# Stacked F32R attention scores with a reordered first mixer, and a second feed-forward that applies the norm's root after its projection

## The chip, the cores and the metric

The kernel runs on one core of one Trainium2 chip. The metric is the device time of one execution in microseconds; less is better. TensorE is called PE here, VectorE DVE, ScalarE ACT, as the profile names them.

## What is computed

Two layers of a hybrid backbone work on 256 latent tokens and 256 context tokens of width 1024. Layer 0 mixes with differential attention (4 heads) and a bidirectional gated linear attention (4 heads), layer 1 with a bidirectional HGRN2 (8 heads). Each layer has a SwiGLU feed-forward of width 2816, and each sub-layer an RMS norm with a scale and a shift from the conditioning vector. Only the latent rows leave layer 1. Cut to what the change touches:

```python
def diff_attend(q, k, v, lam):
    s = jnp.einsum('bqhcd,bkhcd->bhcqk', q, k).astype(F32) * (A_DQK ** -0.5)   # A_DQK = 64, c = 2 channels
    p = jax.nn.softmax(s, axis=-1)
    a = (p[:, :, 0] - lam * p[:, :, 1]).astype(v.dtype)
    return jnp.einsum('bhqk,bkhe->bqhe', a, v)
...
ol = jnp.concatenate([post_a(oa_l), post_b(ob_l, bgl)], axis=-1)     # post_b: rms_norm(o) * silu(g)
x = x + mod_l[2] * (ol @ w_out)
hl = rms_norm(x, norm2_gain[l]) * (1.0 + mod_l[4]) + mod_l[3]
x = x + mod_l[5] * swiglu(hl, w_ffn_in[l], w_ffn_out[l])             # (silu(hl @ Wg) * (hl @ Wu)) @ Wo
```

## The kernel before

Features lie on the 128 partitions (8 tiles `k` of 1024 features), tokens along the free dimension: columns 0 to 255 are context, 256 to 511 latents. Large matrices are multiplied at F32 quality from two F32R parts: a weight piece of 128 x 1024 (8 blocks) comes in as `w`, ACT rounds it to `wH`, DVE makes the rest `wL = w - wH` (`wpiece`, L270 and L271). The activations are split in the same way (`hH`, `hL`). `mm3` then issues three products for a block: `wH` by the high part, `wH` by the low part, `wL` by the high part. `dense_group` loops over `k`, and for each `k` over the output tiles; `dense_wide`, used by layer 1's feed-forward alone, puts a row's high and low part side by side in one 512-column operand, so that a block takes a pair of products, of 512 and of 256 columns, and the two halves of the 512-column result are added later.

A Tile scheduler sets the order on every engine from the program's order, priorities and its own estimate of times; each engine then runs its own list strictly in order. So a product that waits holds back all that stands behind it on PE. Buffers come from pools; those of a tag with one buffer are reused only when the last reader is done. The PSUM pools hold three banks of tag `d` (`dtile`), and two each of tags `a` and `s` and one of `t` (`mtile`).

The first mixer: `qk_tile(which, hd)` projects one head's queries or keys (24 products of 512 columns, except for head 0), takes their mean squares with a product by `c_blk64` (L744), the root by Ln and Exp on ACT, and rotates the latent half. It leaves one F32 tile with channel 0 on rows 0 to 63 and channel 1 on rows 64 to 127; each head has a tile of its own (`x0` to `x7`, the buffers of the residual stream, which is read again from memory afterwards). `attn_head(hd)` makes the scores `s_ps` (L774): context queries against 256 keys, latent queries against 512, in blocks of 128 queries, and for each block and channel one F32 product of 64 rows. DVE takes the maximum, ACT the exponential, DVE combines the channels, PE transposes (`t_ps`) and multiplies by the values (`oa_ps`). `gla_pair(p)` is the linear attention of two heads; its many tiny products (32 and 64 wide) write the tile `a`. `ada(n)` computes adaLN vectors by 32-row products of `ada_w` on PE. The output gate `gs` of the linear attention is 4 dense groups of 24 products, then copied and passed through Silu. `split` makes the high and low part of the mixer's output tiles, `oH` and `oL`; `ov[0..3]` are attention, `ov[4..7]` linear attention. The scheduler interleaves all of these.

Layer 1's end: the HGRN2 heads end with `o_ps`, a normalization on ACT (`hos`), a transposition `ot_ps`, a gate product on DVE (L1142) and the split into `ov` (L1145, L1146). The out projection takes output tiles 0 to 5 in one group and then 6 and 7 in groups of their own. `residual` (L844) adds each result to the residual stream. `token_rstd` sums squares by products with ones (`nms`) and takes the root, `norm_part` multiplies, shifts and splits into `hw`, and `ffn_narrow` starts its first group of four output tiles with `dense_wide`.

Of the kernel before, what the change touches and what calls it, by code (L numbers as in the profile page):

```python
# [51 lines left out]
def hybrid_kernel(ctx: ExitStack, tc: tile.TileContext, A, out, dbg=None):  # L52
# [752 lines left out]
    for hd in range(1, 4):  # L805
        ada(1, "d")
        qT[hd] = qk_tile(0, hd)
        kT[hd] = qk_tile(1, hd)
        ada(1, "d")
        oa[hd] = attn_head(hd)  # L810
    dump("q1", qT[1])
    dump("oa1", oa[1])
# [1 line left out]
    dump("ob1", ob[1])
    dump("ob2", ob[2])
    gs = {}
    for j in range(4):
        gs[j] = bigp.tile([P, T], F32, name=f"gs{j}", tag=f"vB{j}")
        ps = dtile()
        dense_group(fl, [ps], h, range(KT), extra=1, tag="d")  # L820
        V.tensor_copy(out=gs[j], in_=ps)
    for j in range(4):
        S.activation(out=gs[j], in_=gs[j], func=AF.Silu)
# [4 lines left out]
    for hd in range(4):
        V.tensor_tensor(out=ob[hd], in0=ob[hd], in1=gs[hd], op=ALU.mult)
        ov[4 + hd] = split(ob[hd], T, 4 + hd)  # L830
    dump("ob1p", ob[1])
# [360 lines left out]
    for j in range(6):  # L1192
        residual(o6[j], 1, 2, j, xl[j], ssq, halves(256))
# [169 lines left out]
```

## Time and profile before

| | |
|---|---|
| median of 3 runs | 1160.94 us (1158.55 to 1163.29) |
| profiled execution | 1166.56 us, its span 1164.8 us |
| mean granted PE clock | 0.988 |
| busy share PE, DVE, ACT | 98%, 70%, 48% |
| first mixer | about 93 to 303 us of the span |
| layer 0's out projection and feed-forward | about 303 to 700 us |
| layer 1's mixer | about 700 to 958 us |
| layer 1's feed-forward | 973 to 1161 us |

The profile is of one execution of the kernel. Matmuls are pipelined, so the length of one record is more than what it takes in a stream; what a product costs in a stream is the distance from its start to the next start. An F32 product leaves two records, an F32R product one.

### The profile page before, as it was taken

To read this page: it belongs to the slowest core of one execution; us is meant where nothing else is said; L and a number is where in the kernel's file an instruction comes from. 1 tells how busy PE (TensorE), PEld (TensorE's weight loads), DVE (VectorE), ACT (ScalarE), POOL (GpSimd) and SP (SyncE) were. 2 spreads that over 40 slices of the span, in tenths; PEclk is the share of its full clock that TensorE was granted. 3 is DMA by queue.
4 is the path that set the end of the run, shared out by engine and by line. 5 is a ranking of instruction groups with operands and counts; after the bars stand their busy time and mean duration, and the time that the engine had idled before them with its cause. 6 is when DMAs were issued, how large, how long until landed. Compare 5 with 4: busy or idle time off the path is not lost. (4 is left out here: it accounts for less than half of the span.)

```text
span 1164.8 us, 20915 instructions
## 1 busy us (share of the span) xinstructions
PE 1143.3 (98%) x8426; PEld 955.3 (82%) x8426; DVE 816.5 (70%) x1731; ACT 560.2 (48%) x996; POOL 0.2 (0%) x4
## 2 busy tenths in 40 slices
PE   8999989999999999999999999999999998999998
PEld 6777656666799888888888889999898987888887
DVE  3437855995668767666776647869898977776774
ACT  5435535764445222122222225858868865543552
POOL 0000000000000000000000000000000000000000
PEclk9999989999999999999999999999999998999999
DMA  9531431343433555455777521442221233556552
GB/s 359 211 116 36 147 110 37 127 145 124 146 130 109 167 192 160 153 178 181 240 238 245 177 95 55 145 145 92 73 78 69 93 128 109 184 179 199 188 193 91
DMA packets 50017, 170.13 MB, mean 146 GB/s; under 512 B 6528, under 2 KB 8064, under 8 KB 49792
## 3 DMA queue, kind: packets, MB, share of 16 engines
q1 hardware_dynamic: 49920, 168.79, 43.0%
q8 instruction: 66, 1.08, 0.4%
q14 instruction: 31, 0.25, 0.1%
HBM read 167.72 MB, written 1.05 MB: 145 GB/s over the span
## 5 line engine op out<-in xcount | busy, mean ns | idle before, releaser
L270 ACT CAST wH<-w 128x1024 fp32r<-128x1024 f32 x212 | 222.2, 1050 | 387.9 <-PE d L118 272.3
L271 DVE TENSOR_TENSOR wL<-w,wH 128x1024 fp32r<-128x1024 f32 x212 | 258.7, 1222 | 107.0 <-ACT wH L270 104.5
L118 PE MATMUL d<-hH,wH 128*128 128x512 f32 (+1 forms) x800 | 286.4, 365 | 1.6 <-DVE modt L163 1.2
L118 PE MATMUL d<-hL,wH 128*128 128x512 f32 (+1 forms) x800 | 286.2, 358 | 0.0
L118 PE MATMUL d<-hH,wL 128*128 128x512 f32 (+1 forms) x800 | 285.5, 357 | 0.0
L118 PEld LDWEIGHTS d<-hH,wH 128*128 128x128 f32 x800 | 152.1, 191 | 27.7 <-issue 2.6
L118 PEld LDWEIGHTS d<-hL,wH 128*128 128x128 f32 x800 | 151.9, 190 | 21.8 <-issue 1.2
L118 PEld LDWEIGHTS d<-hH,wL 128*128 128x128 f32 x800 | 151.5, 190 | 21.5
L118 PE MATMUL d<-hw,wH 128*128 128x512 f32 x352 | 125.9, 402 | 3.1 <-DVE hw L404 3.1
L118 PE MATMUL d<-hw,wL 128*128 128x256 f32 x352 | 99.3, 282 | 0.0
L228 DVE SCALAR_TENSOR_TENSOR jk<-ada_w,scb 128x1024 bf16<-128x1024 f32 x80 | 97.7, 1222 | 1.6 <-DMA ada_w<-in_w_ada 0.2
L118 PEld LDWEIGHTS d<-hw,wH 128*128 128x128 f32 x352 | 67.3, 191 | 19.9 <-DVE hw L404 3.5
L118 PE MATMUL d<-gH,wH 128*128 128x512 f32 (+1 forms) x198 | 72.2, 366 | 0.0
L118 PE MATMUL d<-gL,wH 128*128 128x512 f32 (+1 forms) x198 | 72.0, 365 | 0.0
L118 PE MATMUL d<-gH,wL 128*128 128x512 f32 (+1 forms) x198 | 72.0, 365 | 0.0
L118 PEld LDWEIGHTS d<-hw,wL 128*128 128x128 f32 x352 | 67.6, 192 | 0.0
L844 DVE SCALAR_TENSOR_TENSOR x<-d,modt,x 128x256 f32<-128x256 f32 x80 | 35.7, 480 | 45.2 <-PE d L118 44.9
L118 PE MATMUL d<-wH,hH 128*128 128x256 f32 (+1 forms) x192 | 61.9, 323 | 0.0
L118 PE MATMUL d<-wL,hH 128*128 128x256 f32 (+1 forms) x192 | 61.6, 322 | 0.0
L118 PE MATMUL d<-gw,wH 128*128 128x512 f32 x176 | 61.5, 396 | 0.0
L118 PE MATMUL d<-wH,hL 128*128 128x256 f32 (+1 forms) x192 | 61.5, 321 | 0.0
L947 DVE TENSOR_TENSOR fs<-fs,d 128x512 f32<-128x512 f32 (+1 forms) x24 | 15.3, 643 | 60.9 <-PE d L118 60.5
(234 smaller groups left out, 1813.7 us busy)
## 6 DMA issues: line engine op xcount, KB each, us to landing
w<-in_w_ffn_in SPq DMA_DIRECT2D x88, 512.0 KB, 3.4
ada_w<-in_w_ada SPq DMA_DIRECT2D x80, 512.0 KB, 4.3
w<-in_w_ffn_out SPq DMA_DIRECT2D x44, 512.0 KB, 3.4
ada_w<-in_w_ada SPq DMA_DIRECT2D x8, 1024.0 KB, 9.2
w<-in_w_even_a SPq DMA_DIRECT2D x16, 512.0 KB, 4.6
w<-in_w_odd_f SPq DMA_DIRECT2D x16, 512.0 KB, 3.3
x<-in_xT SPq DMA_DIRECT2D x16, 256.0 KB, 3.8
w<-in_w_out_even SPq DMA_DIRECT2D x8, 512.0 KB, 3.7
```

Of the source, the lines that this page charges most:

```text
L118: return PE.matmul(out=o, lhsT=l, rhs=r, start=start, stop=stop)
L228: ins = V.scalar_tensor_tensor(out=jk, in0=w1[0], scalar=1.0, in1=scb[:, v, :], op0=ALU.mult, op1=ALU.mult, accum_out=modt[:, l, m, dt, v: ...
L270: cast = S.copy(out=wH, in_=w)
L271: ins = V.tensor_tensor(out=wL, in0=w, in1=wH, op=ALU.subtract)
L844: tail[0] = V.scalar_tensor_tensor(out=xt[:, lo:hi], in0=ps[:, lo:hi], scalar=mods[l, m, k][:, v:v + 1], in1=xt[:, lo:hi], op0=ALU.mult, o ...
L947: V.tensor_tensor(out=s[:, lo:hi], in0=s[:, lo:hi], in1=pu, op=ALU.mult)
```

## The change

1. Scores. `qk_tile` now splits its result: for channel `c`, `qs[c]` holds the rounded queries of the channel on its own 64 rows and their remainder on the other 64 rows; `kh[c]` holds the rounded keys on both row halves, `kl[c]` the remainder on both. A score is `qs[c]` by `kh[c]` plus `qs[c]` by `kl[c]`, two F32R products over 128 rows. For the queries that is one ACT copy and one DVE subtraction of 64 rows and 512 columns per channel, for the keys two and two. These six tiles have one buffer each for all heads (tags `x0` to `x5`), and the F32 result has one per `which` (`x6`, `x7`).
2. Order of the first mixer. Attention of heads 1 and 2, then head 3's queries and keys, then `gla_pair(1)`, then all of `gs`, with attention of head 3 after that in the program but at a raised priority. `gs` is now x times Exp(-Ln(1 + Exp(-x))), without Silu. The linear attention's outputs are gated and split first, and the out projection of layer 0 takes its `k` in the order 4 to 7, 0 to 3.
3. Layer 1's out projection is one group over all eight output tiles. After each residual, ACT and DVE make `hu`: the residual stream times the norm's per-feature scale, split into a high and a low part, without the root. Two more columns of `hu`, 256 and 257, hold the shift.
4. `ffn_narrow` projects `hu` with `dense_group`: three products of 258 columns for each block. The root is computed beside the first group. `act` multiplies the 256 columns by the root on DVE and adds column 256 as the shift's projection: as the bias of Silu for the gate, as the first scalar of the product for the other half.

```diff
-        t = xp.tile([P, T], F32, name=f"qk{which}{hd}", tag=f"x{2 * hd + which}")
+        t = xp.tile([P, T], F32, name=f"qk{which}{hd}", tag=f"x{6 + which}")
...
+        for c in range(2):
+            own, far = (slice(0, 64), slice(64, 128))[::1 - 2 * c]
+            if which == 0:
+                a = xp.tile([P, T], F32R, name=f"qs{c}", tag=f"x{c}")
+                S.copy(out=a[own], in_=t[own])
+                V.tensor_tensor(out=a[far], in0=t[own], in1=a[own], op=ALU.subtract)
+                parts.append(a)
+            else:
+                a = xp.tile([P, T], F32R, name=f"kh{c}", tag=f"x{2 + 2 * c}")
+                b = xp.tile([P, T], F32R, name=f"kl{c}", tag=f"x{3 + 2 * c}")
+                for r in (own, far):
+                    S.copy(out=a[r], in_=t[own])
+                for r in (own, far):
+                    V.tensor_tensor(out=b[r], in0=t[own], in1=a[own], op=ALU.subtract)
+                parts.append((a, b))
+        return parts
...
-                    mm(sp_[:, 0:nkeys], q[r, q0:q0 + P], k[r, 0:nkeys], True, True)
+                    for i in range(2):
+                        mm(sp_[:, 0:nkeys], q[c][:, q0:q0 + P], k[c][i][:, 0:nkeys], i == 0, i == 1)
...
+            S.activation(out=e, in_=ps, func=AF.Exp, scale=-1.0)
+            V.tensor_scalar(out=e, in0=e, scalar1=2.0 ** 63, scalar2=None, op0=ALU.min)
+            S.activation(out=e, in_=e, func=AF.Ln, bias=one_t)
+            S.activation(out=e, in_=e, func=AF.Exp, scale=-1.0)
+            V.tensor_tensor(out=e, in0=ps, in1=e, op=ALU.mult)
...
     gla_pair(1)
+    gs_all()
+    with tc.high_priority(offset=400):
+        oa[3] = attn_head(3)
     load_x()
+    for hd in range(4):
+        gate_ob(hd)
+        ov[4 + hd] = split(ob[hd], T, 4 + hd)
     for hd in range(4):
         ov[hd] = split(oa[hd], T, hd)
...
-    dense_group(flo, pss, ov, range(KT))
+    dense_group(flo, pss, ov, OUT_KS)
...
-                S.copy(out=gb, in_=pg[:, 256:512])
-                V.tensor_tensor(out=gb, in0=gb, in1=pg[:, 0:256], op=ALU.add)
-                S.activation(out=s, in_=gb, func=AF.Silu)
-                S.copy(out=u, in_=pu[:, 256:512])
-                V.tensor_tensor(out=u, in0=u, in1=pu[:, 0:256], op=ALU.add)
-                V.tensor_tensor(out=s, in0=s, in1=u, op=ALU.mult)
+                    for i, (o, ps) in enumerate(((gb, pg), (u, pu))):
+                        V.tensor_copy(out=add[:, i:i + 1], in_=ps[:, 256:257])
+                        V.tensor_tensor(out=o, in0=ps[:, 0:256], in1=rsd, op=ALU.mult)
+                    S.activation(out=s, in_=gb, func=AF.Silu, bias=add[:, 0:1])
+                    V.scalar_tensor_tensor(out=s, in0=u, scalar=add[:, 1:2], in1=s, op0=ALU.add, op1=ALU.mult)
...
-                        pss = [dtile(), dtile(), dtile(), mtile("d3", "s")]
-                        dense_wide(fin, pss, hs, range(KT))
+                        pss = [mtile("d0", "s"), mtile("d1", "s"), mtile("d2", "t"), dtile()]
+                        dense_group(fin, [ps[:, 0:258] for ps in pss], hu, range(KT))
+                        rsd = norm()
...
-    dense_group(flo, o6, ov, range(KT), 2)
...
+    dense_group(flo, o8, ov, range(KT), 2)
+    low = {}
+    for j in range(KT):
+        residual(o8[j], 1, 2, j, xl[j], None, halves(256))
+        if j >= 2:
+            after(tail[0], [low[j - 2]])
+        a = acoef[1, 1, j][:, 1:2]
+        S.activation(out=hu[j][0][:, 0:256], in_=xl[j], func=AF.Identity, scale=a)
+        low[j] = V.scalar_tensor_tensor(out=hu[j][1][:, 0:256], in0=xl[j], scalar=a, in1=hu[j][0][:, 0:256],
+                                        op0=ALU.mult, op1=ALU.subtract)
```

The scheduler's lists change at the places below. A row has the line, the operation, output and inputs, the output's shape, and how often it stands in a row.

PE at the end of layer 1's out projection, before. `d<-ov` are its last products, `nms` the norm's sums, `d<-hw` the feed-forward's first pair.

```order
L118 MATMUL d<-ov_9672,wH 128x256 x2
L118 MATMUL d<-ov_9672,wL 128x256
L118 MATMUL nms<-ssq,ones 128x256
L118 MATMUL nms<-nsq,ones 128x256 x2
L118 MATMUL d<-hw_9957,wH 128x512
L118 MATMUL d<-hw_9957,wL 128x256
```

The same place after:

```order
L119 MATMUL d_9805<-ov_9787,wH 128x256
L119 MATMUL d_9805<-ov_9787,wL 128x256
L119 MATMUL d_9805<-ov_9787,wH 128x256 x2
L119 MATMUL d_9805<-ov_9787,wL 128x256
L119 MATMUL d_10093<-hu,wH 128x258
L119 MATMUL d_10094<-hu,wH 128x258
L119 MATMUL d_10095<-hu,wH 128x258
L119 MATMUL d<-hu,wH 128x258
```

The norm's sums no longer stand between the two; each of the four now stands among the products of the first feed-forward groups. Ahead of this place, between the last head's `o_ps` and its transposes `ot_ps`, there were 15 products of the out projection and 66 after them; now there are 43, and 40 after the first transpose.

PE at the hand-over from head 1's last scores to head 2's first, before (`qk` tiles, two heads' buffers apart):

```order
L118 MATMUL s_ps<-qk_1790,qk_1746 128x512
L118 MATMUL d<-ada_w,sc 32x128 x14
L118 MATMUL oa_ps<-aT,vA_1512 128x256
L118 MATMUL oa_ps<-aT,vA_1514 128x256
L118 MATMUL d<-ada_w,sc 32x128 x2
L162 MATMUL d<-ident,ada_ev 128x128 x2
L118 MATMUL s_ps<-qk_2041,qk_1997 128x256
```

The same hand-over after (`qs`, `kh`, `kl`: one buffer each; the first pair is channel 1 of head 1, the second channel 0 of head 2):

```order
L119 MATMUL s_ps<-kh_1835,qs_1782 128x512
L119 MATMUL s_ps<-kl_1836,qs_1782 128x512
L119 MATMUL d<-hH_625,wL 128x512
L119 MATMUL oa_ps<-aT,vA_1530 128x256
L119 MATMUL oa_ps<-aT,vA_1532 128x256
L119 MATMUL s_ps<-kh_2106,qs_2056 128x256
L119 MATMUL s_ps<-kl_2107,qs_2056 128x256
```

Each score has become two products, and head 2's first scores follow head 1's last ones closely.

DVE ahead of that place, before (the rotation of head 2's keys, `qk_2041`, which its scores read):

```order
L748 SCALAR_TENSOR_TENSOR qk_2041<-d,c_qkg,qsq 128x512
L750 STREAM_SHUFFLE sh<-qk_2041 128x256
L679 TENSOR_TENSOR ls<-mn,ls 128x512
L751 TENSOR_TENSOR sh<-sh,c_rope 128x256
L752 TENSOR_TENSOR qk_2041<-qk_2041,c_rope 128x256
L163 TENSOR_REDUCE modt<-d 128x4
L271 TENSOR_TENSOR wL<-w,wH 128x1024
L775 TENSOR_REDUCE st<-s_ps 128x1
L585 SCALAR_TENSOR_TENSOR bb<-one_t,ls 128x256 x2
L781 RECIPROCAL st<-st 128x2
L753 TENSOR_TENSOR qk_2041<-qk_2041,sh 128x256
```

The same after, from the row on that ends the first `wL`:

```order
L272 TENSOR_TENSOR wL<-w,wH 128x1024
L675 TENSOR_SCALAR mn<-g_ps,c_b_up 128x512
L578 SCALAR_TENSOR_TENSOR bb<-one_t,ls 128x256 x2
L754 TENSOR_TENSOR qk_2099<-qk_2099,sh 128x256
L167 TENSOR_TENSOR modt<-modt,bada 128x4
L272 TENSOR_TENSOR wL<-w,wH 128x1024
L164 TENSOR_REDUCE modt<-d 128x4
L625 SCALAR_TENSOR_TENSOR oa_1592<-oa_1592,sgain,hsq 128x512
L800 RECIPROCAL st<-st 128x2
L170 SCALAR_TENSOR_TENSOR modt<-modt,ngain 128x4
L771 TENSOR_TENSOR kl_2107<-qk_2099,kh_2106 64x512 x2
```

Before, head 2's keys were ready with the rotation's last addition; now the two subtractions for `kl` come after it, behind a second `wL` and a 512-wide multiplication of the attention output.

More of the change, by code (lines that the diff above doesn't have):

```diff
@@ L798, in hybrid_kernel, with gs_all, gate_ob @@
     oa = {}
+    ov = {}
+    gs = {}
+    def gs_all():
+        for j in range(4):
+            gs[j] = bigp.tile([P, T], F32, name=f"gs{j}", tag=f"vB{j}")
+            ps = dtile()
+            dense_group(fl, [ps], h, range(KT), extra=1, tag="d")
+            e = gs[j]
+            S.activation(out=e, in_=ps, func=AF.Exp, scale=-1.0)
[3 more added lines that the diff above has]
+            V.tensor_tensor(out=e, in0=ps, in1=e, op=ALU.mult)
+    def gate_ob(hd):
+        V.tensor_tensor(out=ob[hd], in0=ob[hd], in1=gs[hd], op=ALU.mult)
     qT[0] = qk_tile(0, 0, pss[4])
@@ L804, in hybrid_kernel @@
     oa[0] = attn_head(0)
[L805 to L812, printed above, removed]
-    gla_pair(1)
[L814 to L823, printed above, removed]
+    ada(1, "d")
+    qT[1] = qk_tile(0, 1)
+    kT[1] = qk_tile(1, 1)
+    ada(1, "d")
+    oa[1] = attn_head(1)
+    ada(1, "d")
+    qT[2] = qk_tile(0, 2)
+    kT[2] = qk_tile(1, 2)
+    ada(1, "d")
+    oa[2] = attn_head(2)
+    ada(1, "d")
+    qT[3] = qk_tile(0, 3)
+    kT[3] = qk_tile(1, 3)
+    ada(1, "d")
+    gla_pair(1)
+    gs_all()
+    with tc.high_priority(offset=400):
+        oa[3] = attn_head(3)
     load_x()
-    ov = {}
+    for hd in range(4):
+        gate_ob(hd)
+        ov[4 + hd] = split(ob[hd], T, 4 + hd)
     for hd in range(4):
         ov[hd] = split(oa[hd], T, hd)
[L828 to L831, printed above, removed]
     ada_until(3)
@@ L886, in hybrid_kernel, with ffn_narrow @@
         ps = dtile()
-        dense_group(flo, [ps], ov, range(KT))
+        dense_group(flo, [ps], ov, OUT_KS)
         residual(ps, 0, 2, j, x[j], ssq, halves(T))
-    h, *closing = close_norm(flo, ov, range(KT), 0, 2, x, ssq, 0, 1)
+    h, *closing = close_norm(flo, ov, OUT_KS, 0, 2, x, ssq, 0, 1)
     dump("x1", x[1])
-    def ffn_narrow(xs, gpool, hs, win, wout, final):
+    def ffn_narrow(xs, gpool, win, wout, final, hu, norm):
         fin = Flat(win)
@@ L1188, in hybrid_kernel, with norm @@
     flo = Flat(A["w_out_odd"])
[L1189 to L1202 removed]
+    hu_t = nps.tile([P, 2, KT, 258], F32R, name="hu", tag="hu", bufs=1)
+    sh_ = modt[:, 1, 3, :, 1:2].to_broadcast([P, KT, 2])
+    S.copy(out=hu_t[:, 0, :, 256:258], in_=sh_)
+    V.tensor_tensor(out=hu_t[:, 1, :, 256:258], in0=sh_, in1=hu_t[:, 0, :, 256:258], op=ALU.subtract)
+    hu = {k: (hu_t[:, 0, k], hu_t[:, 1, k]) for k in range(KT)}
+    pss = [dtile(), dtile(), dtile(), mtile("d3", "a")]
+    o8 = [pss[j // 2][:, (j % 2) * 256:(j % 2) * 256 + 256] for j in range(KT)]
+    dense_group(flo, o8, ov, range(KT), 2)
[8 more added lines that the diff above has]
+                                        op0=ALU.mult, op1=ALU.subtract)
+    sums = []
+    for j in range(0, KT, 2):
+        sq = [nps.tile([P, 256], F32, name="nsq", tag="nsq", bufs=5) for _ in range(2)]
+        for i in range(2):
+            S.activation(out=sq[i], in_=xl[j + i], func=AF.Square)
+        V.tensor_tensor(out=sq[0], in0=sq[0], in1=sq[1], op=ALU.add)
+        sums.append(sq[0])
+    def norm():
+        return token_rstd(sums, 0, 256)
     ges = ExitStack()
@@ L1303, in host_arrays @@
     wo = _blocks(f["w_out_odd"][0])
[L1304 to L1305 removed]
+    o["w_out_odd"] = _pieces(_group(wo, range(KT), range(KT)))
     for l in range(2):
```

31 lines of the change are left out of this document (10 added, 21 removed).

## The prediction

> **What bounds the kernel.** I read the page's first part, then TensorE's waits, then the table of stretches with the granted clock, then the chain that ended last, and only then single rows.
>
> ```profile
> span 1164.8 us, 20915 instructions
> PE 1143.3 (98%) x8426; PEld 955.3 (82%) x8426; DVE 816.5 (70%) x1731; ACT 560.2 (48%) x996; POOL 0.2 (0%) x4
> ```
>
> PE is the bound: it has no work in only 2% of the span. Two things can therefore help: less PE work, or fewer waits of PE.
>
> ```profile
> PE a L118 <- issue: 3.8, 1, 3.8
> PE d L118 <- DVE hw L404: 3.1, 1, 3.1
> PE d L118 <- ACT ov L1145: 1.2, 1, 1.2
> PE d L118 <- DVE modt L163: 1.2, 1, 1.2
> PE nms L118 <- DVE ssq L384: 0.9, 1, 0.9
> PE ot_ps L640 <- ACT hos L634: 0.7, 1, 0.7
> PE d L118 <- ACT qsq L72: 0.7, 1, 0.7
> PE d L118 <- issue: 0.5, 1, 0.5
> PE s_ps L118 <- ACT p L72: 0.5, 1, 0.5
> ```
>
> The columns after the colon are total us, times, longest. `hw`, `ov`, `nms` and `ot_ps` stand at the end of layer 1's mixer: 3.1 + 1.2 + 0.9 + 0.7 = 5.9 us. The two `issue` rows, `modt`, `qsq` and `s_ps` stand in the first mixer: 3.8 + 0.5 + 1.2 + 0.7 + 0.5 = 6.7 us. The waits have a second price, which the table of stretches shows (stretch: its length, then busy time of PE, PEld, DVE, ACT, POOL, then granted clock):
>
> ```profile
> 142.80:146.20 3.40, 3.40 (x10) 2.63 (x9) 3.19 (x16) 1.54 (x5) 0.00 (x0) 0.50 0.00 0
> 166.70:176.90 10.20, 8.78 (x31) 5.48 (x31) 4.60 (x19) 2.02 (x5) 0.00 (x0) 0.50 0.20 66
> 200.00:260.00 60.00, 59.53 (x608) 39.26 (x608) 55.03 (x183) 41.40 (x96) 0.00 (x0) 1.00 0.39 135
> 371.00:693.00 322.00, 322.00 (x1423) 266.63 (x1422) 216.72 (x330) 79.71 (x90) 0.00 (x0) 1.00 0.56 185
> 717.30:756.60 39.30, 39.30 (x329) 39.27 (x328) 31.19 (x61) 32.43 (x55) 0.00 (x0) 1.00 0.34 112
> 958.60:962.00 3.40, 3.40 (x18) 3.40 (x18) 1.94 (x5) 1.22 (x3) 0.00 (x0) 0.50 0.30 116
> 973.25:979.10 5.85, 5.85 (x18) 4.98 (x19) 3.91 (x10) 2.06 (x5) 0.00 (x0) 0.50 0.00 0
> 979.10:1160.90 181.80, 181.80 (x1040) 158.07 (x1038) 127.56 (x203) 85.07 (x130) 0.00 (x0) 1.00 0.53 173
> ```
>
> After each cluster of waits the granted clock is 0.50 for 3.4 to 10.2 us, and half of such a stretch is lost: in the first mixer (3.4 + 10.2) / 2 = 6.8 us. So a wait of 1 to 2 us costs 3 to 4. The Trainium skill ("TensorE: Matmul & The Clock Gate", Part 1) says the clock falls back only after an idle window of about 3.4 us. The trace differs: 0.7 + 1.2 us ahead of 142.8 were enough. By the page new short waits would cost only themselves; I go by the rows.
>
> The same table prices PE's products. In 371 to 693 only 512-column products run: 322.0 / 1422 = 0.2264 us each. In 717 to 757 only 256-column ones: 39.3 / 328 = 0.1198. From 979 on `dense_wide`'s pairs run (512 and 256 columns): 181.8 / 520 = 0.3496 a pair.
>
> **Part 1, scores on stacked halves.** A score product was one F32 product over 64 rows, and is now two F32R products over 128 rows (`kh`, then `kl`). Before, by rows of groups (mean ns) and of the timeline (start, length):
>
> ```profile
> L118 PE MATMUL s_ps<-qk,qk 64*128 64x512 f32 x32 | 14.5, 638 | 0.0
> L118 PE MATMUL s_ps<-qk,qk 64*128 64x256 f32 x32 | 8.9, 463 | 0.5 <-ACT p L72 0.5
> 135.61 1.13 PE L118 MATMUL s_ps<-qk,qk 64*128 64x512 f32 x4
> 136.67 0.44 PE L162 MATMUL d<-ident,ada_ev 128*128 128x128 f32 x2
> 149.00 1.12 PE L118 MATMUL s_ps<-qk,qk 64*128 64x512 f32 x2
> 150.06 0.50 PE L118 MATMUL d<-hH,wH 128*128 128x512 f32 x1
> 160.40 0.70 PE L118 MATMUL s_ps<-qk,qk 64*128 64x256 f32 x4
> 161.03 0.64 PE L118 MATMUL d<-ada_w,sc 128*32 128x128 f32 x14
> 205.84 0.70 PE L118 MATMUL s_ps<-qk,qk 64*128 64x256 f32 x2
> 206.47 0.50 PE L118 MATMUL d<-hH,wH 128*128 128x512 f32 x1
> ```
>
> A product leaves two records, so there are 16 of each width. Start to next start, one 512-wide score takes 150.06 - 149.00 = 1.06 us, and two that stand side by side (x4) take 136.67 - 135.61 = 1.06 together: the halves at rows 0 and 64 overlap. For 256 it is 0.63 and 0.63. PE's order has 3 pairs and 10 single ones of 512, 5 pairs and 6 single of 256: 13 x 1.06 + 11 x 0.63 = 20.7 us. After: 32 x 0.2264 + 32 x 0.1198 = 11.1 us. Gain 9.6 us. Its bounds: if each new product, standing among F32 work, took twice its streaming time, 22.2 us and nothing gained; a larger gain than 9.6 nothing allows. I take 9.6, since dense products stand around most of them. A rule that speaks against this part is in the Trainium skill (same page, Part 3): products over few rows in different row groups run concurrently. The trace agrees where two stand side by side. By the rule for all 16 pairs the old scores would cost 8 x 1.06 + 8 x 0.63 = 13.5 us and the gain 2.4; the rows show that most do not stand so.
>
> For this DVE gets 24 subtractions of 512 columns, ACT 24 copies.
>
> ```profile
> L596 DVE TENSOR_TENSOR kd<-kd,qkb 128x512 f32<-128x512 f32 x2 | 1.4, 686 | 0.0
> L271 DVE TENSOR_TENSOR wL<-w,wH 128x1024 fp32r<-128x1024 f32 x15 | 18.3, 1220 | 5.5 <-ACT wH L270 5.4
> L748 DVE SCALAR_TENSOR_TENSOR qk<-d,c_qkg,qsq 128x512 f32<-128x512 f32 x8 | 6.0, 748 | 6.4 <-ACT qsq L72 6.4
> 139.21 0.60 ACT L72 ACTIVATE qsq<-d 128x512 f32<-128x512 f32 x1 [2.23 <-PE d L118]
> ```
>
> DVE: 24 x 0.69 = 16.5 us; ACT: 24 x 0.6 = 14.4. The stretch 200 to 260 shows DVE busy 55.0 of 60 us, ACT 41.4: ACT has room, DVE hardly. Three heads' share there is 18 x 0.69 = 12.4 us. It is covered only because gla_pair(1) is stretched over more of PE's work, and because 260 to 300 has slack.
>
> **Part 2, the new order of the first mixer.** `q` and `k` parts now have one set of buffers, so a head's parts wait for the last scores of the head before. At the hand-over to head 2 (order rows in the section on the change) the `kl` of channel 0 is the last of 18 DVE rows from the 0.75 us multiplication of `qk` on, with two `wL` (2 x 1.22) among them; taken at the length per column of the rows above they are 11.3 us. `c_blk`'s F32 product (1.06, like a score) and two ACT steps (0.6 each) come before: 13.5 us. PE has beside that 24 dense products (5.4 us), three F32 products of 512 (3.2) and two of 256 (1.3), two scores (0.9) and, as an estimate from the rest of the table, 1.8 of adaLN pieces and transposes: 12.6. So about 1 us shows. The code stretch with the 3.8 us `issue` wait (two runs of 56 tiny products with adaLN pieces between) is still there, nearly row for row, and I expect it back. Waits of this mixer before: 6.7 idle + 6.8 of clock = 13.5. I take +1.5 against that. Bounds: -13.5 (all old waits gone) and +16.5 (all new DVE work shown).
>
> gs's silu by Exp and Ln (ACT 12 steps instead of 4), the gates and splits of `ob` first: costed at nothing, because 96 dense products (21.7 us) and then the out projection's first 36 (8.2 us) run over them. If that cover fails, a chain of some 5 us (three ACT steps of 0.6, four DVE steps of 0.69) shows before the out projection.
>
> **Part 3, layer 1's out projection and norm.**
>
> ```profile
> 951.54 2.05 PE o_ps L118 x16
> 957.90 9.78 PE d L118 x66
> 968.58 1.58 PE nms L118 x6
> 973.25 187.67 PE d L118 x1056
> 956.08 0.59 PE L640 MATMUL ot_ps<-ident,hos 128*128 128x128 f32 x2 [0.69 <-ACT hos L634]
> 957.45 0.40 ACT L1145 CAST ov<-gs 128x256 fp32r<-128x256 f32 x1 [1.16 <-DVE gs L1142]
> L844 DVE SCALAR_TENSOR_TENSOR x<-d,modt,x 128x256 f32<-128x256 f32 x80 | 35.7, 480 | 45.2 <-PE d L118 44.9
> ```
>
> The first four rows are of the chain, two of the timeline, one of the page's groups. From the last `o_ps` to the first feed-forward product: 973.25 - 951.54 = 21.7 us. After the change PE has there `o_ps` (2.0), the two transposes (0.3) and by the order 83 products of the one group: 83 x 0.1198 = 9.9; together 12.2. The last head's chain (956.08 - 953.6 = 2.5 us from `o_ps` to the transposes, 957.90 - 956.67 = 1.2 from them to `ov`) now has 43 and then 15 products beside it, 5.2 and 1.8 us, so both waits go. The first feed-forward product needs only the first residual (0.48), one ACT step like 957.45's (0.40) and for its low half one DVE step (0.48): 1.4 us, begun while the last 12 products (1.4 us) run. Gain 9.5. The half-clock stretch 973.25 to 979.10 goes too: 2.9. Four norm products now stand inside the feed-forward, at 1.58 / 3 = 0.53: -2.1. Net 10.3 us. What is late next: `rsd` must be ready when the first group's tiles are to be freed; a wait of 1 to 2 us is possible there. Bounds: 12.4 (the norm's products free), and 5 (2 us of wait and 3.4 of clock come back).
>
> **Part 4, feed-forward of 258 columns.** 352 blocks, 3 products instead of a pair. A product of 258: 0.1198 + 2 x (0.2264 - 0.1198) / 256 = 0.1206. Cost: 352 x (3 x 0.1206 - 0.3496) = +4.3 us. Bounds: 0.1198 (+3.4), and, no row having 258 columns, the 512 row's 0.2264 (+116); two columns from 256 I take the slope. `act` loses two ACT copies and gains two one-column copies on DVE; DVE, at 127.6 of 181.8 us there, covers it.
>
> **Sum**: -9.6 + 1.5 - 10.3 + 4.3 = -14.1 us. The profiled execution (1164.8 span, 1166.6 in all) is 5.6 us above the median of 1160.94; I subtract from the median: 1146.8.
>
> **Rivals.**
> 1. The code stall does not come back (it waits for nothing the profile shows, and there is one among eight such runs): -3.8 and half of 10.2, 1146.8 - 8.9 = 1138.
> 2. DVE becomes the bound of the mixer: each of three hand-overs shows 2 us and costs 1.7 of clock: 1146.8 - 1.5 + 11 = 1156, no change. DVE's 55 of 60 us speaks for it, the slack after 260 against.
> 3. The other side: the single set of buffers stops PE. If at each hand-over PE had only the 24 dense products left to run, 3 x (13.5 - 5.4) = 24 us plus 3 x 1.7 of clock: 1146.8 - 1.5 + 29 = 1174. It decides once the mixer's waits grow by 21 us over before (15.6 gained elsewhere, 5.8 for half a per cent). Against it: most rows put 24 dense and more between.
> 4. A 258-column product falls off the 256 rate: 1% more a product is 1.3 us; it decides at +0.02 us each (1056 x 0.02 = 21 us).
>
> **Chances.** Forecast (1140 to 1155) 0.63, rival 1 0.13, rival 2 0.13, rival 3 0.09, rival 4 0.02. Half a per cent, 5.8 us, is what a measurement of this kernel tells from no change. Faster 0.63 + 0.13 = 0.76; same 0.13; slower 0.11. The range 1136 to 1161 leaves out rivals 3 and 4 and part of 1 and 2; its ends are rival 1's time less 2, and the forecast with nearly all DVE work shown.
>
> **What would show it.** `s_ps` near 11 us in all; no `hw`, `ov` or `nms` wait over 0.5 and a clock of 1.00 from 955 of the old count on; feed-forward blocks of 0.362 us; 3 to 6 waits of 0.5 to 1.5 us in the mixer, with DVE above 0.9 busy. Wrong if the mixer's waits pass 20 us, if products of 258 columns are not 0.121, or if a wait for `rsd` or `hu` puts the half clock back at the feed-forward's start.

## The result, and the profile after

The changed kernel takes 1154.2 us (median of 9 runs, 1150.6 to 1157.6) against 1162.1 of the kernel before, run beside it (9 runs, 1158.6 to 1163.9). The ratio is 0.9927, interval 0.9912 to 0.9942: 8.5 us less. A second series later gave 1154.2 again (ratio 0.9929, 0.9912 to 0.9947). The forecast was 1146.8, 14.1 less: the sign is right, about 60% of the size came. 1154.2 lies inside the forecast's 1140 to 1155, 0.8 us from its upper end.

The first part of the page after:

```profile
span 1148.8 us, 21705 instructions
PE 1127.4 (98%) x8780; PEld 970.0 (84%) x8780; DVE 833.9 (73%) x1795; ACT 563.5 (49%) x983; POOL 0.2 (0%) x4
```

PE is busy 15.9 us less, and still 98% of the span. This pair of profiles flatters the change: the execution shown is the fastest of nine, and the one shown of before (1166.6) is above all but one of the 81 runs of that kernel beside the experiments. What differs is the clock. Each timed run comes with its mean granted clock, so its time can be split into time x clock (what it would take at full clock) and time x (1 - clock) (what the half clock took). The two right-hand columns are means over the runs. The row of before has the 69 runs beside e1 to e11; the 12 beside e12 give 1152.2 and 9.6. One execution of e4, 1603.8 us at a granted clock of 0.65, is left out as slow; it is the one that was profiled, so e4 has no trace to compare.

| kernel | runs | median us | at full clock | lost to the clock |
|---|---|---|---|---|
| before | 69 | 1162.4 | 1152.3 | 9.9 |
| changed, both series | 15 | 1154.2 | 1148.7 | 5.1 |
| e1 feed-forward part only | 12 | 1157.9 | 1152.6 | 5.4 |
| e2 mixer part only | 12 | 1157.7 | 1148.5 | 8.9 |
| e3 scores in the old order | 6 | 1171.3 | 1155.3 | 15.8 |
| e4 new order, old scores | 11 | 1159.5 | 1150.3 | 8.9 |
| e5 one group, root not deferred | 12 | 1164.6 | 1152.6 | 11.8 |
| e6 hybrid feed-forward | 6 | 1154.0 | 1148.6 | 6.0 |
| e7 parts on GpSimd | 6 | 1167.5 | 1153.0 | 15.0 |
| e9 `kl` on 64 rows | 5 | 1152.9 | 1149.6 | 3.0 |
| e10 row groups | 12 | 1159.8 | 1150.1 | 10.0 |
| e11 row groups and hybrid | 12 | 1162.2 | 1149.8 | 12.9 |
| e12 `kl` half zero | 7 | 1155.7 | 1149.7 | 6.3 |

Of the 8 us, 3.6 are work and waits and 4.8 are clock, by the means. The rows of after that answer to those of before: PE's waits first (total us, times, longest).

```profile
PE d L119 <- ACT qsq L73: 4.1, 4, 1.9
...
PE d L119 <- DVE modt L164: 2.4, 1, 2.4
PE t_ps L807 <- ACT hsq L73: 1.7, 1, 1.7
PE a L119 <- issue: 1.7, 1, 1.7
PE t_ps L807 <- issue: 1.3, 1, 1.3
...
PE d L119 <- DVE hu L1244: 0.5, 1, 0.5
```

`hw`, `ov`, `nms` and `ot_ps` are gone, as forecast. In the first mixer two have grown, `qsq` from 0.7 to 4.1 and `modt` from 1.2 to 2.4, `hsq` (1.7) is new, and the `issue` rows have shrunk from 4.3 to 3.0. Two stretches, columns as in the prediction; the first runs from the first `kd_ps` of the linear attention to layer 0's first 512-column feed-forward product, the second is layer 1's feed-forward. Before:

```profile
117.36:370.98 253.62, 246.59 (x2391) 181.74 (x2390) 179.62 (x503) 133.98 (x271) 0.00 (x0) 0.97 0.35 119
973.25:1160.63 187.38, 187.38 (x1056) 163.05 (x1056) 131.46 (x213) 87.14 (x134) 0.00 (x0) 0.98 0.51 168
```

After:

```profile
116.62:360.37 243.75, 232.27 (x2388) 180.99 (x2387) 195.03 (x535) 143.87 (x294) 0.00 (x0) 0.99 0.37 124
952.68:1144.68 192.00, 191.37 (x1416) 182.67 (x1416) 140.41 (x265) 82.50 (x103) 0.00 (x0) 1.00 0.53 170
```

The reader is to see the difference of the first two columns, PE's idle time: 253.62 - 246.59 = 7.0 us before, 11.5 after. PE does 14.3 us less there, of which (3.4 + 10.2 - 3.4) / 2 = 5.1 is clock and 9.2 work; DVE has 15.4 us more to do in a stretch that is 10 us shorter.

### The profile page after: what moved, and what is told of

It reads as the page before. It is cut to its first block, busy times and chain, and to the rows that moved or that the text cites. A ratio compares the mean times of both kernels' runs of the same rounds, so it can differ in the third digit from the quotient of the medians.

```text
span 1148.8 us, 21705 instructions
## 1 busy us (share of the span) xinstructions
PE 1127.4 (98%) x8780; PEld 970.0 (84%) x8780; DVE 833.9 (73%) x1795; ACT 563.5 (49%) x983; POOL 0.2 (0%) x4
## 4 chain that ended last, share of the span: by engine, by line
PE 90%; DVE 3%; DMA 3%; ACT 2%; issue 1%; SPq 1%; DVEq 0%; ACTq 0%
PE d L119 79%; PE a L119 3%; PE o_ps L119 2%; DMA w<-in_w_even_a 2%; PE st_ps L119 1%; PE s_ps L119 1%; PE oa_ps L119 1%; DVE wL L272 1%; DMA ada_w<-in_w_ada 1%; ACT wH L271 1%; ACT QK L73 1%; SPq L107 1%; PE ms_ps L119 1%; PE t_ps L807 0%; DMA c_lam<-in_lam 0%
## 5 line engine op out<-in xcount | busy, mean ns | idle before, releaser
L119 PE MATMUL d<-hH,wH 128*128 128x512 f32 (+1 forms) x800 | 283.2, 361 | 1.1 <-ACT qsq L73 0.8
L119 PEld LDWEIGHTS d<-hL,wH 128*128 128x128 f32 x800 | 151.3, 189 | 21.2 <-issue 0.9
L119 PE MATMUL d<-hu,wH 128*128 128x258 f32 x704 | 128.7, 284 | 0.7 <-DVE hu L1244 0.5
L119 PEld LDWEIGHTS d<-hu,wH 128*128 128x128 f32 x704 | 109.2, 189 | 1.6 <-DVE hu L1244 0.7
L119 PE MATMUL d<-hu,wL 128*128 128x258 f32 x352 | 98.9, 283 | 0.0
L119 PEld LDWEIGHTS d<-hu,wL 128*128 128x128 f32 x352 | 66.4, 189 | 0.1
```

Source lines behind the costliest of these rows:

```text
L119: return PE.matmul(out=o, lhsT=l, rhs=r, start=start, stop=stop)
```

## The experiments

Each was timed against the kernel before on the same chip. Since a scheduler makes the lists, an edit also moves rows around it; that is said where it matters.

**e1: the feed-forward part alone** (parts 3 and 4 on the old mixer). Its edit is the last third of the diff above, from the row `S.copy(out=gb, ...)` on: the feed-forward and the one-group out projection.

> Parts 3 and 4 alone on the old first mixer. Theory A (the forecast's terms add): 10.3 us gained at layer 1's out projection, 4.3 lost in the feed-forward, 6.0 us faster than before, about 1156. Theory B (the mixer is what gave less than forecast, through new waits in a typical execution): the same 5 to 6 us here. Theory C (the out projection's gain was only in the profiled execution, whose half clock was longer than usual): 2 to 3 us, about 1159.5.

Measured: 1157.9 us, ratio 0.9961 (0.9947 to 0.9975), -4.6. From the last `o_ps` to the first feed-forward product it takes 12.53 us, as in the whole change (21.71 before; the forecast said 12.2). At full clock nothing is gained (1152.6 against 1152.3): what the shorter stretch brings, the 258 columns and the norm's products take. The whole gain is half clock that no longer falls there (9.9 us lost before, 5.4 here). The size, -4.6 with an interval of about 1.6 either way, does not decide between the theories' 5 to 6 and 2 to 3.

**e2: the mixer part alone** (parts 1 and 2, the first two thirds of the diff).

> Parts 1 and 2 alone, layer 1 as before. Theory A: 8.1 us faster than before, about 1154. Theory B: 2 to 3 us faster, about 1159.5, with the mixer's waits and half clock differing from execution to execution. Theory C: 5 to 6 us faster.

Measured: 1157.7, ratio 0.9958 (0.9942 to 0.9975), -4.9. With e1 that makes -9.5, about the whole (-8.5): no sign that the two disturb each other, and both fall short of their forecasts, the mixer by more (-4.9 of -8.1). That is nearest to theory C's 5 to 6 here, but theory C's 2 to 3 for e1 did not come. At full clock the mixer gains 3.8 (1152.3 to 1148.5), in half clock 1.0.

**e3: stacked scores in the old order.**

```diff
+                for r in (own, far):
+                    V.tensor_tensor(out=b[r], in0=t[own], in1=a[own], op=ALU.subtract)
...
+                        mm(sp_[:, 0:nkeys], q[c][:, q0:q0 + P], k[c][i][:, 0:nkeys], i == 0, i == 1)
```

> Stacked scores alone, in the old order of the mixer, layer 1 as before. If PE's work decides: 9.6 us less of it, and waits as in the changed order, 6 to 9 us faster than before. If the splits' DVE and ACT work needs the new order to be covered: no faster than before, with longer waits of PE in the mixer.

Measured: 1171.3, ratio 1.0076 (1.0054 to 1.0098): 8.8 us slower than before. PE's waits, and the out projection's start:

```profile
PE d L118 <- DVE oH L646: 5.0, 1, 5.0
PE d L118 <- ACT qsq L72: 4.1, 4, 1.9
...
PE ms_ps L118 <- ACT hsq L72: 2.9, 1, 2.9
PE d L118 <- DVE modt L163: 2.4, 1, 2.4
```

```profile
308.70:318.90 10.20, 5.09 (x10) 2.38 (x9) 6.08 (x12) 6.07 (x8) 0.00 (x0) 0.50 0.70 286
```

PE does the same smaller work as after (below), but in the old order the attention heads' outputs come last, and their normalization (`hsq` 2.9) and split (`oH` 5.0) show right ahead of the out projection; 10.2 us of half clock follow. The waits for `qsq` (4.1) and `modt` (2.4) are those of the changed kernel, so they come with the scores and not with the new order. Slower than before is the side of the forecast's third rival, but not by its mechanism: it had PE stop at the hand-overs between heads, and the long new waits stand ahead of the out projection.

**e4: the new order with the old F32 scores** (the rows of the diff from `gs` to `OUT_KS`).

> New order of the mixer, with gs by Exp and Ln and the out projection's order, but the old F32 scores and their old buffers. If the order itself is worth nothing: within 2 us of before. If the order is what pays and the stacked scores give it back: 5 to 8 us faster. PE's work is the same as before, so any difference is waits and half clock.

Measured: 1159.5, ratio 0.9978 (0.9962 to 0.9994), -2.6. So the order is worth some 2.6, and the scores some 2.3 on top of it (a difference of two runs whose intervals overlap); alone the scores cost 8.8. They are no two terms that can be added. At full clock e2 is 1.8 us under e4 (1148.5 against 1150.3), although e4's PE still has the F32 scores' work, which in the old order was about 9 us more.

**e5: one out projection group, root not deferred.**

```diff
+    o8 = [pss[j // 2][:, (j % 2) * 256:(j % 2) * 256 + 256] for j in range(KT)]
+    dense_group(flo, o8, ov, range(KT), 2)
...
     norm_part(1, 1, ...)
```

> The kernel before with one edit: layer 1's out projection is one group over all eight output tiles; norm, root and the paired feed-forward stay as before. Theory A (the gain at this place comes from the deferred root, the one group only allows it): the waits ot_ps 0.7 and ov 1.2 go, but all eight residuals now end together and hw's wait grows from 3.1 to 4 to 6 us with the half clock behind it; from the last o_ps to the first feed-forward product 20 to 23 us (21.7 before, 12.5 after); time 1160 to 1164 against 1162.5. Rival B (the one group alone covers the last head and the norm): that stretch 13 to 16 us, time 1155 to 1157.

Measured: 1164.6, ratio 1.0024 (1.0013 to 1.0035): some 3 us slower. Two of PE's waits:

```profile
PE nms L118 <- DVE ssq L384: 5.8, 1, 5.8
PE d L118 <- DVE hw L404: 3.1, 1, 3.1
```

The one group covers the last head, as in the change, and then all eight residuals end together: the sum of squares is 5.8 us late instead of 0.9, the stretch takes 24.3 us (half clock in it). Theory A holds in kind; stretch and time lie just above its 23 and 1164, and the new wait came at `nms`, while `hw` stayed at 3.1. The deferred root is what makes the one group pay.

**e6: a hybrid feed-forward.** Output tiles 0 to 7 use `hu`, all later ones the normed rows in pairs.

```diff
+                if half == 0 and j == 2:
+                    norm_part(1, 1, ..., xs, rsd, halves(256)[0])
+                if half == 1 or j >= JS:
+                    dense_wide(fin, [pg], hw, range(KT))
+                    dense_wide(fin, [pu], hw, range(KT))
...
```

> The changed kernel, but the feed-forward's output tiles 8 to 10 of the first half and all of the second half use the normed rows (made beside the first tiles) in pairs of 512 and 256 columns. Theory A (three 258-column products cost 0.360 us a block against 0.3496 for the pair, whatever stands beside them): 224 blocks x 0.0104 = 2.3 us less than the changed kernel, first feed-forward product to last 189.7 us against 191.9, time 1152. Rival B (the norm's 8 tiles of extra DVE and ACT work hold up the tiles' freeing): 0.5 to 3 us of new waits before tile 8, time as the changed kernel or above.

Measured: 1154.0, no different from the changed kernel. Both theories were right at once. PE's work in that feed-forward falls by 2.2 us (191.5 to 189.3 at full clock), but eight of the sixteen norm steps (`nxn`, `hw`) stand with two `wL` in DVE's list ahead of `fg`, the multiplication that frees the next tile:

```profile
PE d L120 <- DVE fg L954: 3.0, 1, 3.0
```

```profile
972.48 1.67 DVE L402 SCALAR_TENSOR_TENSOR nxn<-x,modt,nrs 128x256 f32<-128x256 f32 x4
...
976.38 1.22 DVE L273 TENSOR_TENSOR wL<-w,wH 128x1024 fp32r<-128x1024 f32 x1
977.52 1.27 DVE L406 SCALAR_TENSOR_TENSOR hw<-nxn,modt,hw 128x256 fp32r<-128x256 f32 x3
...
978.98 0.42 DVE L954 TENSOR_TENSOR fg<-d,nrs 128x256 f32<-128x256 f32 x1
```

```profile
976.50:979.60 3.10, 0.10 (x2) 0.09 (x1) 3.10 (x9) 1.00 (x2) 0.00 (x0) 1.00 0.72 226
980.90:984.40 3.50, 3.50 (x19) 3.50 (x18) 3.50 (x8) 2.48 (x7) 0.00 (x0) 0.52 0.42 137
```

DVE is busy for the whole of the 3.1 us, PE for 0.1; then comes the half clock.

**e7: the score parts on GpSimd.** This asks whether PE's waits for `qsq` and `modt` come from the splits. In the trace of after, the end of PE's wait at 201.5, ACT's rows there, and DVE's rows of the wait at 246.7:

```profile
201.48 0.28 PE L119 MATMUL s_ps<-kl,qs 128*128 128x256 f32 x1
203.61 1.13 PE L119 MATMUL d<-qsq,c_blk 128*128 128x512 f32 x2 [1.86 <-ACT qsq L73]
...
201.04 1.26 ACT L769 CAST kh<-qk 64x512 fp32r<-64x512 f32 x2
202.33 0.61 ACT L762 CAST qs<-qk 64x512 fp32r<-64x512 f32 x1
202.96 0.60 ACT L73 ACTIVATE qsq<-d 128x512 f32<-128x512 f32 x1
...
246.97 1.39 DVE L771 TENSOR_TENSOR kl<-qk,kh 64x512 fp32r<-64x512 f32 x2
248.28 0.68 DVE L763 TENSOR_TENSOR qs<-qk,qs 64x512 fp32r<-64x512 f32 x1
248.88 0.17 DVE L164 TENSOR_REDUCE modt<-d 128x4 f32<-128x16 f32 x1
249.10 1.25 PE L119 MATMUL d<-ada_w,sc 128*32 128x128 f32 x28 [2.38 <-DVE modt L164]
```

PE does not wait for `kh` or `kl`: its scores of the new head at 201 start without a wait. It waits for the small step that stands in the list right behind the splits, `qsq` of 0.60 us and a reduction of 0.17. The splits are not all that stands there. Ahead of `modt` DVE is busy without a gap, with rows of the linear attention (`QK`), a `wL` and softmax steps beside the splits (columns as in the prediction, DVE third of the busy times):

```profile
235.70:248.90 13.20, 11.02 (x84) 7.94 (x77) 13.11 (x36) 9.01 (x19) 0.00 (x0) 1.00 0.38 119
```

```diff
-                S.copy(out=a[own], in_=t[own])
-                V.tensor_tensor(out=a[far], in0=t[own], in1=a[own], op=ALU.subtract)
+                G.tensor_copy(out=a[own], in_=t[own])
+                G.tensor_tensor(out=a[far], in0=t[own], in1=a[own], op=ALU.subtract)
...
```

> The changed kernel with all copies and subtractions that make qs, kh and kl on GpSimd instead of ACT and DVE. Theory A (PE's waits for qsq, 1.9 and 1.0, and for modt, 2.4, come from ACT and DVE standing in their lists behind parts whose buffers the last head's scores still hold): these three waits fall below 0.5 each, 4 to 5 us and one half-clock stretch (1.7) less, time 1148 to 1150 against 1154 of the changed kernel. Rival B (GpSimd needs more than 1.5 us for a 64 x 512 step, so that a head's twelve steps show): s_ps waits of 3 us or more at the three hand-overs, 1160 to 1175. Rival C (the waits are DVE's load in that stretch, not the place of the parts in the lists): waits move but keep their sum of about 11 us, time 1152 to 1156.

Measured: 1167.5, ratio 1.0050 (1.0035 to 1.0065): 13 us slower than the changed kernel. GpSimd's row for one step, and DVE's row for the same step in the trace of after:

```profile
L772 POOL TENSOR_TENSOR kl<-qk,kh 64x512 fp32r<-64x512 f32 x16 | 21.5, 1342 | 0.9
```

```profile
L771 DVE TENSOR_TENSOR kl<-qk,kh x16: 673/686/690, 113.5 to 247.7; 64x512 fp32r<-64x512 f32 x16
```

1342 against 686 ns, about twice. The Trainium skill ("GPSIMD Engine Reference", opening section) says that VectorE is roughly 2x faster at ordinary elementwise work; the trace agrees. The parts come later, and `t_ps` (6.6 us), `issue` (3.5), `s_ps` (2.8), `modt` (2.5) and `qsq` (2.0) wait. Rival B was right in the time, less so in the place; the question itself stays open in this run.

**e8: the changed kernel again**, for a second profile.

> The changed kernel unchanged, for a second profiled execution and its times on the same chip. If the half-clock stretches are set by the program, they come at the same places as in the first profile (one, 3.4 us, after modt's wait at 247). If they depend on how a wait falls in the throttle's own period, PE's waits keep their places and lengths (sum 11 us in the first mixer) while zero to three half-clock stretches of 3.4 us come at different ones; time 1152 to 1156.

Measured: 1154.2. The waits are nearly the same (`qsq` up to 1.9 and `modt` 2.4 again, 10.7 us of idle time after 11.5), the half clock is not. In the first profile:

```profile
247.00:249.60 2.60, 0.50 (x20) 0.50 (x24) 2.56 (x5) 0.00 (x0) 0.00 (x0) 1.00 0.64 207
249.60:253.10 3.50, 3.50 (x34) 2.80 (x23) 3.33 (x18) 2.09 (x6) 0.00 (x0) 0.51 0.90 279
```

In the second, at the same place (the wait there was 2.4 us again) and at an earlier one:

```profile
249.80:253.30 3.50, 2.70 (x42) 2.00 (x43) 3.36 (x17) 1.99 (x6) 0.00 (x0) 1.00 0.85 281
159.10:166.00 6.90, 6.51 (x132) 5.37 (x131) 5.48 (x13) 3.39 (x6) 0.00 (x0) 0.51 0.52 174
```

After one and the same wait for `modt` the clock is 0.51 once and 1.00 the other time; a wait of 1.5 us at 156 is followed by a half-clock stretch in the second, and the same wait, 1.3 us, by none in the first. The second theory holds.

**e9: `kl` on its own 64 rows.**

```diff
-                for r in (own, far):
-                    V.tensor_tensor(out=b[r], in0=t[own], in1=a[own], op=ALU.subtract)
+                V.tensor_tensor(out=b[own], in0=t[own], in1=a[own], op=ALU.subtract)
...
+                    for i, r in enumerate((slice(0, P), slice(64 * c, 64 * c + 64))):
+                        mm(sp_[:, 0:nkeys], q[c][r, q0:q0 + P], k[c][i][r, 0:nkeys], i == 0, i == 1)
```

> The changed kernel with one edit: kl is made on its own 64 rows alone, and the second score product runs over these 64 rows (qh by kl; the remainder of q by the remainder of k is left out). Two of a head's six 64 x 512 subtractions on DVE go, ACT's steps and all PE widths stay. Theory A (PE's wait for modt at 247 is DVE's list: two kl steps 1.39 and one qs step 0.68 stand right ahead of modt's reduction): that wait falls by one kl step, from 2.4 to 1.7, the qsq waits (1.9 and 1.0), which are behind ACT's copies, stay; time 1152 to 1154. Rival B (DVE's whole load makes the waits): with 8 x 0.69 = 5.5 us less work on DVE all of the mixer's 11 us of waits shrink, by 3 us or more, the qsq ones too; time 1149 to 1151.

Measured: 1152.9, ratio 0.9906 (0.9885 to 0.9927), not to be told from the changed kernel. The mixer's stretch, and one score of it:

```profile
118.47:364.24 245.77, 241.27 (x2389) 182.89 (x2388) 190.59 (x525) 145.35 (x294) 0.00 (x0) 0.99 0.36 123
```

```profile
228.97 0.51 PE L119 MATMUL s_ps<-kh,qs 128*128 128x512 f32 x1
229.41 0.49 PE L119 MATMUL s_ps<-kl,qs 64*128 64x512 f32 x1
```

The idle time falls from 11.5 to 4.5 us, `qsq` from 4.1 to 1.0, and `modt` has no row left. That looks like rival B, but the stretch is no shorter, because PE is 9 us busier (1.7 of it half clock). Neither theory had that: 229.41 - 228.97 = 0.44 us from a 128-row to a 64-row product, where two 128-row ones stand 0.23 to 0.34 apart. Over 32 pairs the work rises by 7.3 us, on average 0.1 at each of the 64 changes of rows.

**e10: scores by row groups.** Whole tiles `qh`, `ql`, `kh`, `kl`, three products of 64 rows, the channels in turn.

```diff
+                for i in range(3):
+                    for c in range(2):
+                        r = slice(64 * c, 64 * c + 64)
+                        mm(sps[c][:, 0:nkeys], q[i == 1][r, q0:q0 + P], k[i == 2][r, 0:nkeys], i == 0, i == 2)
```

> The changed kernel with other score parts: a head's queries and keys are rounded as whole 128-row tiles (qh, kh) and the remainders made as whole tiles (ql, kl): 4 ACT and DVE steps a head instead of 12, the keys' tiles in two sets of buffers. A score is three products over 64 rows (qh kh, ql kh, qh kl), the two channels' products issued in turn. Theory A (the splits in the ACT and DVE lists cost the 4.5 us of new waits; products of two row groups overlap where they stand side by side, as F32 ones did): qsq and modt waits below 1 us each, 3 to 5 us of waits less and perhaps a half-clock stretch (1.7); PE's scores by the order (6 of 8 pairs of 256, 3 of 8 of 512 side by side) 6 x 3 x 0.1198 + 2 x 6 x 0.1198 + 3 x 3 x 0.2264 + 5 x 6 x 0.2264 = 12.4 us against 11.1; time 1148 to 1151. Rival B (F32R products of two row groups do not overlap): scores 16.6 us, time 1152 to 1156. Rival C (the waits are not the splits'): waits stay near 11 us, time 1154 to 1157.

Measured: 1159.8, ratio 0.9977 (0.9964 to 0.9990): slower than the changed kernel by 5.6.

```profile
118.13:371.55 253.42, 243.47 (x2421) 185.92 (x2420) 184.40 (x515) 137.41 (x283) 0.00 (x0) 0.96 0.35 119
```

```profile
118.66 0.38 PE L119 MATMUL s_ps<-kh,qh 64*128 64x256 f32 x2
118.88 0.28 PE L119 MATMUL s_ps<-kh,ql 64*128 64x256 f32 x2
119.00 0.28 PE L119 MATMUL s_ps<-kl,qh 64*128 64x256 f32 x2
119.21 0.32 PE L119 MATMUL d<-ada_w,sc 128*32 128x128 f32 x4
```

Side by side, the two channels overlap: the middle pair, two products of 256 columns, takes 0.12 us, what one takes in a stream. The first and the last pair, next to products over all rows, take 0.22 and 0.21. In the Trainium skill ("TensorE: Matmul & The Clock Gate", Part 3) matmuls in distinct row groups run concurrently; the trace agrees for F32R too. But `qsq` at 0.7 and no `modt` wait did not shorten the stretch: DVE has 10.6 us less to do than after, and PE idles for 10.0 us, now at `s_ps` (3.3), `issue` (2.1), `wH` and `wL`; 20.5 us run at half clock. Rival C, at a worse time; by the runs 1.4 of the 5.6 us are work and waits (1150.1 against 1148.7) and 4.9 half clock.

**e11: row groups, and the hybrid with its norm steps spread**, two tiles at each of outputs 3 to 6.

> The row-group scores of the run before, and a feed-forward in which output tiles 0 to 7 of the first half use the unrooted rows in 258 columns and all later ones the normed rows in pairs, the normed rows made two tiles at a time beside outputs 3 to 6, so that DVE has no run of sixteen norm steps (a 3.0 us wait for fg and 3.4 us of half clock in the earlier hybrid). Theory A (a pair is 0.0104 us cheaper than three 258-column products, and the wait was the lump of norm steps): first feed-forward product to last 189 to 190 us against 191.9 of the changed kernel, no wait for fg over 0.5, and 2 us under the row-group kernel's time: 1146 to 1149. Rival B (the norm steps cost PE a wait wherever they stand): a wait of 1 us or more at outputs 3 to 6, time within 1 us of the row-group kernel's.

Measured: 1162.2, ratio 0.9997 (0.9983 to 1.0011). PE waits 3.0 us for `fg` again, at 986: in DVE's list the same eight norm steps and two `wL` stand ahead of it as in e6, so the steps did not come out spread. Rival B's wait came, 2.4 us above the row-group kernel's time, but whether spread steps would cost a wait was not put to the test.

**e12: `kl` with a half of zeros**: DVE's relief of e9 without its 64-row products.

```diff
+                if hd == 0:
+                    kl[c] = xp.tile([P, T], F32R, name=f"kl{c}", tag=f"x{3 + 2 * c}")
+                    V.tensor_tensor(out=kl[c][far], in0=t[own], in1=t[own], op=ALU.subtract)
...
+                V.tensor_tensor(out=b[own], in0=t[own], in1=a[own], op=ALU.subtract)
```

> The changed kernel, with kl's far halves zero for all heads (made once, at head 0) and only its own half subtracted a head: DVE has 8 + 2 instead of 16 kl steps, 6 x 0.69 = 4.1 us less, and the second score product still runs over 128 rows, so PE's products are those of the changed kernel (q's remainder by k's remainder is left out). Theory A (PE's waits of this mixer, 10.6 to 11.5 us, come from ACT's and DVE's lists being full with the splits; the run with kl on 64 rows had 4.5 us of waits but 7.4 us more PE work from switching between 128-row and 64-row products): PE work of the mixer stays at 230 to 231 us, waits fall to 5 to 8 us, no modt wait over 1; time 1147 to 1151. Rival B (the 64-row run's waits fell only because PE itself was slower there): waits stay at 10 to 12 us, time 1153 to 1156.

Measured: 1155.7, ratio 0.9948 (0.9929 to 0.9967).

```profile
117.49:366.71 249.22, 237.34 (x2389) 184.20 (x2388) 190.65 (x529) 145.46 (x294) 0.00 (x0) 0.97 0.35 121
```

DVE has 4.4 us less, `modt` no longer stops PE, and the idle time is 11.9 us: `t_ps` for `p` 2.4, `s_ps` 2.7, `issue` 1.9. Rival B holds in idle time and in time; of theory A only the missing `modt` wait came. Removing a wait moved it.

Put together, the stretch from `kd_ps` to the 512-column products, in us (idle is length less PE busy, clock half of the half-clock stretches, work the rest):

| kernel | work | idle | work + idle | clock |
|---|---|---|---|---|
| before | 239.8 | 7.0 | 246.8 | 6.8 |
| e1, old mixer | 240.4 | 7.4 | 247.8 | 5.1 |
| e3, scores in the old order | 229.0 | 21.2 | 250.2 | 8.5 |
| after | 230.6 | 11.5 | 242.0 | 1.7 |
| after, second profile | 230.4 | 10.7 | 241.1 | 3.4 |
| e2, mixer alone | 230.9 | 12.2 | 243.0 | 3.4 |
| e5, old mixer | 240.9 | 4.7 | 245.6 | 3.4 |
| e6 | 230.4 | 10.9 | 241.3 | 3.4 |
| e9 | 237.9 | 4.5 | 242.4 | 3.4 |
| e10 | 233.2 | 10.0 | 243.2 | 10.2 |
| e12 | 230.5 | 11.9 | 242.4 | 6.8 |

In the new order the stretch lasts 241 to 243 us at full clock whether PE has 230 or 238 us of work, each in one execution. PE's work alone no longer sets that length; DVE's sum does not either (184 to 195 us busy, same length). e4's and e2's runs point the same way (9 us less work, 1.8 us gained). The 238 us rest on e9 alone, which also relieves DVE, so two effects may cancel there. What does set the length is not shown. A chain through the engines' lists would fit; some rows of after's chain, in time order, show it leaving PE:

```profile
202.33 0.61 ACT qs L762
202.96 0.61 ACT qsq L73
203.61 1.14 PE d L119 x2
...
207.45 2.64 ACT QK L73 x7
...
247.67 0.69 DVE kl L771
248.36 0.60 DVE qs L763
249.10 1.47 PE d L119 x32
```

Which order would shorten it was not tried, and stays open.

## Why the prediction was right or wrong

The forecast's terms, parted into full clock and clock (of the 9.5 us of part 3's gap, 2.2 were half clock, and 2.9 stood behind it), and what the profiles show:

| term | forecast | measured |
|---|---|---|
| PE work of the first mixer (part 1) | -9.6 | -9.2 |
| mixer's waits (part 2) | +1.5 | +4.5 idle |
| last `o_ps` to feed-forward, without clock | -7.3 | -7.0 |
| feed-forward with the norm's products | +6.4 | +7.5 |
| ahead of the mixer, and layer 0's feed-forward to layer 1's end | 0 | +0.2 |
| sum at full clock | -9.0 | -4.0 (runs: -3.6) |
| clock at layer 1's end | -5.1 | runs, whole kernel: -4.8 |

- **Part 1 was right in sum, not in its rows, and that is partly luck.** `s_ps` was to be near 11 us; by starts it is 15.8 (21.1 less the 5.3 us of waits behind it). Between dense products a 512-column score takes 0.226, as priced, but beside the tiny products, the adaLN pieces or an F32 product 0.31 to 0.43. By starts and at full clock the scores fall from 21.2 to 15.6 us, 5.6 of the 9.6 forecast. The rest of the 9.2 stands in other rows, for which the forecast had no term: `d<-ada_w` falls from 16.9 to 15.1, `ms_ps` from 6.4 to 5.5. That 64-row scores made their neighbours dearer would fit e9, where these two rise again to 15.7 and 6.1; it was not tested by itself.
- **Part 2 is the step that failed: against its +1.5 the idle time alone rose by 4.5.** Its term counts idle time and half clock together. In the two executions first profiled that sum hardly moves (13.9 to 13.2 us), but the half clock differs from execution to execution; by the runs, e2 came 4.9 us faster with 8.9 us less of PE's work, so the two together rose by some 4. The forecast asked when `kl` is ready for the scores, found 13.5 against 12.6 us of cover, and let 1 us show at `s_ps`. There nothing showed. The splits stand as blocks in ACT's and DVE's lists, and an in-order list holds up what stands behind them: `qsq` and `modt`, on which PE's next rows hang. That the single set of buffers is what puts the blocks there is argued, not shown: in the rows at 201 and 247 ACT and DVE go from one step to the next without waiting for a buffer. Rival 2, three hand-overs of 2 us each, names the size better (1.9, 1.0 and 2.4); it gave 1156, and the result is nearer to it than to the forecast. DVE's load, rival 2's reason, fits the `modt` wait, which is gone in e9, e10 and e12, the three kernels that relieve DVE. For the sum of the idle time it does not fit: with 10.6 and 4.4 us less on DVE, e10 and e12 still idle for 10.0 and 11.9.
- **Of the forecast's gain of part 1, about half became waiting**: PE's 9.2 us less work made the stretch 4.8 shorter at full clock (246.8 to 242.0; the executions of each spread by 2 us). Something else holds the stretch at about 242 us, 2 us above what PE alone had to do there before, and the prediction had no term for it.
- **Part 3 was right**: 12.53 us against 12.2, no wait for `ov`, `nms` or `hw`, and the half clock gone there. With part 4's price it gains nothing at full clock, so that e1's 4.6 us are the clock term (-5.1) alone. The wait it feared came at `hu`, 0.5 us.
- **Part 4 was right**: two columns more cost nothing that can be seen or the slope.

```profile
1050.43:1113.69 63.26, 63.26 (x527) 63.26 (x528) 0.00 (x0) 0.00 (x0) 1.00 0.56 184
```

63.26 / 528 = 0.1198 us for a 258-column product, the figure of the 256-column row; in the first half 50.80 / 419 = 0.1212. Of the +7.5, 0.5 is `hu`'s wait and some 0.6 I cannot place.
- **The code stall**, the forecast's name for the `issue` wait, was expected back at 3.8 us with 10.2 of half clock. It came as 1.7 and 1.3 in the first profile and 0.6 and 1.5 in the second; on the old mixer it is 4.4 in e1 and 2.0 in e5. Its length is not fixed by the rows, and what causes it no run shows.
- **The base.** The sum was made against the profiled execution and taken off the median. Its clock terms held on average, but one profile could not show it: the same programs lose 9.9 and 5.1 us to the clock on average, and 14.0 and 2.3 in the two executions first profiled. That a wait of 1 to 2 us costs 3 to 4 is so in some executions only (e8).

## What to carry to other kernels

When work is taken off the bounding engine, look for the length of the stretch without it: here work + idle stayed at 241 to 243 us, and about half of what was saved became a wait. Price a split also by what stands behind it in the in-order list, not only by when its own reader needs it. A change that defers a step may gain nothing in work and still pay by taking away the waits that bring the half clock; that gain must be read from many runs' clocks, not from one profile.
